# A hybrid decoder layer: ten early weight tiles for the down stage, later token sums, and halves' differences on VectorE

## The chip, the cores and the metric

The kernel runs on one core of one Trainium2 chip, as one launch. The metric is the device time of that launch in microseconds (us); lower is better. A core has five engines that run side by side: TensorE (PE, matmuls into PSUM), VectorE (DVE), ScalarE (ACT), GpSimd (POOL) and SyncE (SP), which here only issues DMAs. DMAs are also issued from GpSimd's queue. All of them share sixteen DMA engines.

## What is computed

One decoder layer on 512 tokens of 1024 channels, in float32. The first sub-layer mixes tokens (RWKV-7 and native sparse attention side by side); the change does not touch it. The second is a gated MLP with a short causal convolution between the up-projection and the gate:

```python
x = x + rms_norm(m @ w_out, norm_mix_post)
h = rms_norm(x, norm_ffn_pre)
u = causal_dwconv(h @ ffn_up, ffn_conv_w, ffn_conv_b)   # width 3, per channel
u_gate, u_val = split(u, 2)                             # 2816 = 22 x 128 each
x = x + rms_norm((silu(u_gate) * u_val) @ ffn_down, norm_ffn_post)
```

## The kernel before

Every matrix is held as a high and a low part (a value rounded to the matmul format, made by a copy on ScalarE, and the rest, made by a subtraction), and each product takes three matmuls: high x high, high x low, low x high. So each weight tile of 128 x 512 costs one DMA of 256 KB into a raw tile, one ScalarE copy (`hi`), one subtraction on VectorE or GpSimd (`lo`), and then its matmuls.

**Up stage** (the loop `for j in range(22)`). Pair j makes 128 gate channels and 128 value channels: two blocks of matmuls, the convolution (one ScalarE and two VectorE instructions for each block, L1619 to L1621), SiLU on ScalarE, the product of both, and its split into `ah[:, j]` (L1638) and `al[:, j]` (L1639). There are two kinds of pairs:

- *Ordinary pairs*, j = 0 to 9: full products with loaded weights (`split_w`, tiles `up..`, line L172 for the rest). The product of gate and value runs on GpSimd (L1630). For j < 11 (`KH`) the right half of the tokens is then replaced by right half less left half (L1637); in ordinary pairs this runs on GpSimd too.
- *Token-half pairs*, j = 10 to 21 (`SEVEN`): a seven-product scheme over halves of the channels and of the tokens (`seven`, L1567 for its matmuls, L1572 for its additions on VectorE, L1578 for its copy). Its weights `sw..` are loaded tiles and sums of tiles that were formed in memory beforehand. Product and difference run on VectorE. For j from 11 on, three more VectorE subtractions make a tile `t24`, which a DMA stores in memory as `t24d[j - 11]` (L1645, the last one from GpSimd's queue, L1652). The pool `t2` that holds `t24` exists from pair 11 to the end of the loop.

**Weight sums** (`ws`): the sums of weight tiles that both seven-product schemes need are formed in memory by DMAs from GpSimd's queue, 48 for the up stage (L251) and then 48 for the down stage (`down_sums`, L272), a plain copy for the first addend and an adding DMA for the second. The generator `ws` is advanced at places written by hand. In the loop above that is once or twice in each ordinary pair and, in token-half pairs, at every even j; in the down stage it is once at every third tile.

**Down stage**: again seven products, `down(m, f, r, n, ..)` for m = 0 to 6, in the order written at the end of the function. Each pass goes over 11 weight tiles (k) and two groups of 128 tokens, three matmuls each (L1730 to L1732). Tiles are numbered n = 0, 1, 2, .. through all passes (`ring`): pass 0 takes 0 to 10, pass 1 takes 11 to 21, and so on; passes 2 to 5 read sums (`ds`). `down_w` allocates and issues a tile: `hi` and `lo` of n = 0 to 2 lie in the ring `whi`/`wlo`, those of later tiles in eight slots of `h2h`/`h2l`, the up stage's input, slot (n - 3) % 8. Raw tiles lie in `wp` (four buffers, shared with the up stage's weights) or in the pool `ep` (four buffers, tag `draw`), which is opened after the pools of the up stage are closed and so lies on their room.

```python
p_, tag, b = (wp, "raw", RAWB) if n < 8 or n % 8 >= 4 else (ep, "draw", 4)
raw = p_.tile([128, 512], F32, tag=tag, name=f"dw{n}r", bufs=b)
load, high = sy.dma_start(raw, src), sc.activation(hi, raw, AF.Copy)
...
low = (po if n % 3 == 1 else ve).tensor_tensor(lo, raw, hi.bitcast(F32), op=OP.subtract)
```

**Token sums** (`turn`): passes 5, 4 and 6 need other token combinations than `ah`/`al` hold. The generator `turn` loads `t24d` back in three chunks of 4, 4 and 3 tiles (L1682; 1024, 1024 and 768 KB), forms for each chunk `ah - t24 + al` in two VectorE instructions (L1690, L1692), and `put` writes the result over `ah` and `al` (L1677 on ScalarE, L1678 on VectorE). It is advanced after the tiles k that `TURN[m]` lists for pass m.

**Order of the work.** The programming layer plans each engine's order with costs of its own; a later instruction can come ahead of an earlier one when its room and inputs are there. `keep` (`tc.keep_in_program_order`) pins an instruction behind everything written before it on its engine. Down tiles from n = 8 on, all chunk loads, sums and `put`s are pinned. Waits for a tile's room are for that tile's former users. Within an engine all runs in order, and a waiting instruction holds up those behind it.

Of the kernel before, what the change touches and what calls it, by code (L numbers as in the profile page):

```python
# [10 lines left out]
F32 = mybir.dt.float32  # L11
F32R = mybir.dt.float32r
AF = mybir.ActivationFunctionType
OP = mybir.AluOpType
# [17 lines left out]
RB = 4  # L32
KH, TL = 11, 4
DCH = tuple(slice(i, min(i + 2, KH)) for i in range(0, KH, 2))
TURN = ((), (0, 4, 6, 7, 8, 10), (1, 3, 4, 6, 8, 9), (3, 6, 9), (2, 5, 8), (), ())
TCH = (slice(0, 4), slice(4, 8), slice(8, 11))
WU = 2
NT = 6
# [14 lines left out]
def hybrid_layer(ctx: ExitStack, tc: tile.TileContext, a, out, dbg=None, stop=None):  # L53
# [1425 lines left out]
    with pool("ff") as ff:  # L1479
# [113 lines left out]
        for j in range(22):  # L1593
            us = []
            sv_ = None
            if j == 2:
                sw = pool("sw", "right", sctx2)
            if j == SEVEN[0]:
                for _ in side:
                    pass  # L1600
            if j in SEVEN:
                sv_ = seven(j)
            for x in range(2):
                blk = 2 * j + x
                if blk < NU:
                    p = pu4[blk]
                    half_up(blk, 1)
                elif sv_ is not None:
                    p = sv_[x]
                else:  # L1610
                    wh, wl = after.get(blk) or split_w(upw(blk), f"up{blk}")
                    p = ((pj, px, py, pz)[blk % 4] if j < SEVEN[0] else pj)(f"pu{blk}")
                    mm3(p, wslice(wh), wslice(wl), lambda k: h2h[:, k, :], lambda k: h2l[:, k, :])
                if blk == 2 * SEVEN[0] - 1:
                    for _ in range(5):
                        next(coming)
                cv = blk * 4
                u = fu.tile([128, S], F32, tag=f"u{x}", name=f"u{blk}", bufs=2)
                sc.activation(u, p, AF.Identity, scale=cvec[:, cv + 2:cv + 3], bias=cvec[:, cv + 3:cv + 4])  # L1619
                ve.scalar_tensor_tensor(u[:, 1:], p[:, :S - 1], cvec[:, cv + 1:cv + 2], u[:, 1:], op0=OP.mult, op1=OP.add)  # L1620
                ve.scalar_tensor_tensor(u[:, 2:], p[:, :S - 2], cvec[:, cv:cv + 1], u[:, 2:], op0=OP.mult, op1=OP.add)  # L1621
                us.append(u)
                if j < SEVEN[0]:
                    for _ in range(1):
                        next(side, None)
                if (j > 2 or x == 0 if j < SEVEN[0] else x + j % 2 == 0):
                    next(ws, None)
            if sv_ is None:
                sc.activation(us[0], us[0], AF.Silu)
                po.tensor_tensor(us[1], us[0], us[1], op=OP.mult)  # L1630
                y = us[1]
            else:
                sc.activation(sv_[0], us[0], AF.Silu)
                y = sv_[1] if j >= KH else us[1]
                ve.tensor_tensor(y, us[1], sv_[0], op=OP.mult)
            if j < KH:
                (po if sv_ is None else ve).tensor_tensor(y[:, rgt], y[:, rgt], y[:, lft], op=OP.subtract)  # L1637
            sc.activation(ah[:, j, :], y, AF.Copy)  # L1638
            ve.tensor_tensor(al[:, j, :], y, ah[:, j, :].bitcast(F32), op=OP.subtract)  # L1639
            if j >= KH:  # L1640
                if j == KH:
                    t2ctx = ExitStack()
                    t2 = pool("t2", "left", t2ctx)
                else:
                    sy.dma_start(t24d[j - 1 - KH], t24)  # L1645
                t24 = t2.tile([128, S], F32, tag="t24", name=f"t24{j}", bufs=2)
                ve.tensor_tensor(t24[:, lft], y[:, rgt], ah[:, j - KH, rgt].bitcast(F32), op=OP.subtract)
                ve.tensor_tensor(t24[:, lft], t24[:, lft], al[:, j - KH, rgt].bitcast(F32), op=OP.subtract)
                ve.tensor_tensor(t24[:, rgt], y[:, lft], t24[:, lft], op=OP.subtract)
            if j == 1:  # L1650
                f4ctx.close()
        po.dma_start(t24d[21 - KH], t24)  # L1652
        t2ctx.close()
        sctx2.close()
        fuctx.close()
        with pool("ep") as ep:
# [23 lines left out]
            def turn():  # L1680
                def load(c):
                    keep(sy.dma_start(t24[:, c], t24d[c].rearrange("k p f -> p k f")))  # L1682

                load(TCH[0])
                yield
                load(TCH[1])
                yield
                for c in TCH:
                    x = ep.tile([128, 4, 256], F32, tag="tt", name=f"tt{c.start}", bufs=1)[:, :c.stop - c.start]
                    keep(ve.tensor_tensor(x, tok(ah, 0, 0, c).bitcast(F32), t24[:, c, lft], op=OP.subtract))  # L1690
                    yield
                    keep(ve.tensor_tensor(x, x, tok(al, 0, 0, c).bitcast(F32), op=OP.add))  # L1692
                    yield
                    put(x, 0, 0, c)
                    yield
                    if c is TCH[0]:
                        load(TCH[2])
                        yield
                for c in TCH:
                    put(t24[:, c, lft], 0, 1, c)  # L1700
                    yield
                for c in TCH:
                    put(t24[:, c, rgt], 1, 0, c)
                    yield

            turned = turn()
            ring = itertools.count()

            def down_w(f, k):
                n = next(ring)  # L1710
                src = a["down4"][f[0], f[1], k] if isinstance(f, tuple) else dsum[k // 2][f][k % 2]
                if n < WB:
                    hi, lo = (wp.tile([128, 512], F32R, tag=t, name=f"dw{t}{n}", bufs=WB) for t in ("whi", "wlo"))
                else:
                    hi, lo = (y[:, (n - WB) % 8, :] for y in (h2h, h2l))
                p_, tag, b = (wp, "raw", RAWB) if n < 8 or n % 8 >= 4 else (ep, "draw", 4)
                raw = p_.tile([128, 512], F32, tag=tag, name=f"dw{n}r", bufs=b)
                load, high = sy.dma_start(raw, src), sc.activation(hi, raw, AF.Copy)  # L1718
                if n >= 8:
                    keep(load)  # L1720
                    keep(high)
                low = (po if n % 3 == 1 else ve).tensor_tensor(lo, raw, hi.bitcast(F32), op=OP.subtract)  # L1722
                if n >= 8:
                    keep(low)
                return hi, lo

            def mms(p, r, n, k, i, w, first, last):
                ks = slice(n * 256 + i * 128, n * 256 + i * 128 + 128)
                xh, xl = (y[:, r * KH + k, ks] for y in (ah, al))
# [4 lines left out]
            def down(m, f, r, n, bank, side=iter(())):  # L1734
                p = [bank(f"dn{m}{i}") for i in range(2)]
                for k in range(KH - TL if m == 6 else KH):
                    w = down_w(f, k)
                    for i in range(2):
                        mms(p[i], r, n, k, i, w, k == 0, k == KH - 1)
                    if k in TURN[m]:  # L1740
# [155 lines left out]
```

## Time and profile before

| | us |
|---|---|
| median of 3 runs | 1151.74 (1150.83 to 1154.2) |
| profiled execution | 1148.3 |
| its span, first to last instruction | 1146.5 |
| TensorE busy | 1116.8 (97%) |
| VectorE busy | 739.3 (64%) |
| ScalarE busy | 639.3 (56%) |
| GpSimd busy | 623.4 (54%) |
| first matmul of the token-half pairs / of the down stage, from the span's start | 900.96 / 1023.25 |

The time is that of a whole launch; the profiled execution is one of its own, and its span leaves out what lies before the first and after the last instruction. In the rows below, "L1722" is line 1722 of the kernel before, `hl<-dw16r,hh` is what an instruction writes and reads, and a bracket at the end of a row says how long its engine stood idle before it and what ended that. In rows by stretch, "PEclk" is the clock that TensorE was granted, as a part of the full one.

### The profile page before, as it was taken

To read this page: it belongs to the slowest core of one execution; us is meant where nothing else is said; L and a number is where in the kernel's file an instruction comes from. 1 tells how busy PE (TensorE), PEld (TensorE's weight loads), DVE (VectorE), ACT (ScalarE), POOL (GpSimd) and SP (SyncE) were. 2 spreads that over 40 slices of the span, in tenths; PEclk is the share of its full clock that TensorE was granted. 3 is DMA by queue.
4 is the path that set the end of the run, shared out by engine and by line. 5 is a ranking of instruction groups with operands and counts; after the bars stand their busy time and mean duration, and the time that the engine had idled before them with its cause. 6 is when DMAs were issued, how large, how long until landed. Compare 5 with 4: busy or idle time off the path is not lost.

```text
span 1146.5 us, 21236 instructions
## 1 busy us (share of the span) xinstructions
PE 1116.8 (97%) x7704; PEld 910.9 (79%) x7704; DVE 739.3 (64%) x1420; ACT 639.3 (56%) x1258; POOL 623.4 (54%) x627
## 2 busy tenths in 40 slices
PE   9999999999999999999999999999999999998997
PEld 7888888777888787666676778889778899996685
DVE  4236655735665653687787745754873699986886
ACT  6447764554666334576775554444454567654644
POOL 4346765545765554566555535531678877743331
PEclk9999999999999999999999999999999999999999
DMA  7524568543665897336575466685558677879583
GB/s 265 138 72 122 154 169 226 149 121 96 183 145 172 236 255 194 95 105 185 182 196 174 111 165 194 200 300 132 161 166 200 214 227 226 241 192 312 191 288 116
DMA packets 117002, 208.33 MB, mean 182 GB/s; under 512 B 37025, under 2 KB 39905, under 8 KB 110754
## 3 DMA queue, kind: packets, MB, share of 16 engines
q1 hardware_dynamic: 93538, 144.05, 39.9%
q0 software_dynamic: 7504, 48.50, 18.5%
q10 hardware_dynamic: 15856, 14.42, 4.0%
q8 instruction: 61, 1.00, 0.3%
q14 instruction: 43, 0.35, 0.1%
HBM read 179.60 MB, written 72.35 MB: 220 GB/s over the span
## 4 chain that ended last, share of the span: by engine, by line
PE 81%; DVE 7%; DMA 4%; POOL 4%; ACT 3%; issue 2%; SPq 0%; ACTq 0%; DVEq 0%; POOLq 0%
PE sg L1567 4%; PE st L1567 4%; PE gt L348 3%; PE o L1218 3%; PE gt L349 3%; PE gt L350 3%; PE pt L150 3%; PE ub L1276 3%; PE ub L1278 2%; PE ub L1277 2%; PE pu L234 2%; PE pu L232 2%; PE pu L233 2%; PE v L348 2%; PE v L349 2%; PE dn L1731 2%
## 5 line engine op out<-in xcount | busy, mean ns | idle before, releaser
L1166 ACT ACTIVATE p<-p,stt 128x384 f32<-128x384 f32 (+3 forms) x128 | 70.6, 554 | 33.6 <-DVE stt L1164 33.0
L1164 DVE CUSTOM_DVE_ANT_0 p<-s,rh 128x384 f32<-128x384 f32 (+3 forms) x128 | 59.2, 484 | 22.0 <-PE s L1150 18.4
L1731 PE MATMUL dn<-hl,ah 128*128 128x512 f32 x148 | 59.3, 401 | 2.9 <-POOL hl L1722 1.5
L1138 POOL TENSOR_SCALAR p<-p,stt 128x512 f32<-128x512 f32 (+1 forms) x64 | 39.5, 626 | 38.8 <-DVE stt L1131 24.0
L1730 PE MATMUL dn<-hh,ah 128*128 128x512 f32 x148 | 57.5, 395 | 2.8 <-ACT hh L1718 2.7
L1732 PE MATMUL dn<-hh,al 128*128 128x512 f32 x148 | 58.3, 394 | 0.0
L150 PE MATMUL pt<-ident,p 128*128 128x128 f32 x320 | 44.3, 273 | 1.3 <-DVE p L1140 1.2
L1157 PE MATMUL s<-kst,qs 128*128 128x512 f32 (+1 forms) x128 | 38.8, 394 | 6.0 <-DVE stt L1164 5.8
L150 PEld LDWEIGHTS pt<-ident,p 128*128 128x128 f32 x320 | 37.8, 141 | 6.9 <-DVE p L1140 1.6
L1218 PE MATMUL o<-PT,vt 128*64 128x384 f32 (+3 forms) x256 | 41.0, 443 | 0.0
L1731 PEld LDWEIGHTS dn<-hl,ah 128*128 128x128 f32 x148 | 28.2, 190 | 12.1 <-DVE hl L1722 3.9
L1730 PEld LDWEIGHTS dn<-hh,ah 128*128 128x128 f32 x148 | 27.8, 189 | 10.3 <-ACT hh L1718 4.7
L1209 ACT ACTIVATE PT<-pt 128x512 f32<-128x512 f32 x48 | 27.5, 587 | 10.4 <-PE pt L150 10.3
L1157 PEld LDWEIGHTS s<-kst,qs 128*128 128x128 f32 x128 | 21.2, 189 | 15.2 <-DVE stt L1164 11.9
L1732 PEld LDWEIGHTS dn<-hh,al 128*128 128x128 f32 x148 | 28.2, 191 | 5.6
L1140 DVE TENSOR_SCALAR p<-p,stt 128x512 f32<-128x512 f32 (+1 forms) x64 | 31.9, 526 | 0.7
L1218 PEld LDWEIGHTS o<-PT,vt 128*64 128x64 f32 x256 | 16.4, 136 | 18.3 <-issue 16.0
L1638 ACT ACTIVATE ah<-u 128x512 fp32r<-128x512 f32 x11 | 7.0, 632 | 40.9 <-POOL u L1637 40.6
L272 POOL DMA_DIRECT2D ds<-in_down_dram x36 | 25.6, 711 | 6.9 <-DMA ds<-ds 6.0
L1211 DVE COPY PT<-pt 128x512 f32<-128x512 f32 x32 | 21.7, 680 | 8.6 <-PE pt L150 8.5
L1639 DVE TENSOR_TENSOR al<-u,ah 128x512 fp32r<-128x512 f32 x11 | 9.2, 837 | 26.5 <-ACT ah L1638 26.5
L251 POOL DMA_DIRECT2D fs<-in_up_dram x36 | 26.1, 731 | 0.5 <-issue 0.4
(2203 smaller groups left out, 4247.0 us busy)
## 6 DMA issues: line engine op xcount, KB each, us to landing
fs<-in_up_dram POOLq DMA_DIRECT2D x36, 512.0 KB, 6.2
ds<-in_down_dram POOLq DMA_DIRECT2D x30, 512.0 KB, 6.0
fs<-fs POOLq DMA_DIRECT2D x12, 512.0 KB, 4.5
ds<-ds POOLq DMA_DIRECT2D x10, 512.0 KB, 5.1
gtd<-gt ACTq DMA_DIRECT2D x16, 256.0 KB, 3.5
qs<-qd SPq DMA_DIRECT2D x32, 128.0 KB, 3.8
g<-gtd SPq DMA_DIRECT2D x16, 256.0 KB, 3.4
t24d<-t SPq DMA_DIRECT2D x10, 256.0 KB, 4.9
```

What stands on the lines that cost most here:

```text
L150: return te.transpose(o, i, ident)
L348: te.matmul(p, wh(k), hh[:, k, :], start=k == 0, stop=False)
L349: te.matmul(p, wh(k), hl[:, k, :], start=False, stop=False)
L1138: po.tensor_scalar(o.pe[e, b, k], o.pe[e, b, k], w, 1.0, op0=OP.mult, op1=OP.mult)
L1157: m = te.matmul(s_[:, :n], qt, kt[:, x, b, :n], start=x == 0, stop=x == 1)
L1164: ve.tensor_tensor_reduce(sb, parts[b], rh[e][:, (3 - qb) * 128:], -1.0, BIG, OP.add, OP.min, st[e][:, 0, i:i + 1])
L1166: sc.activation(sb, sb, AF.Exp, scale=-1.0, bias=st[e][:, 0, i:i + 1], accum_out=st[e][:, 1, i:i + 1])
L1218: te.matmul(acc[e * 64:e * 64 + 64, j * 128:], vt[:, j, b * 256 + g * 64:b * 256 + g * 64 + 64], m[e][:, c:c + n], start=False, stop=k == ...
L1567: te.matmul(p, w[y][:, ks], x[z][:, k, :], start=first and k + n == 0, stop=last and k == hf - 1 and n == 2, skip_group_check=True)
L1730: te.matmul(p, xh, w[0], start=first, stop=False)
L1731: te.matmul(p, xh, w[1], start=False, stop=False)
L1732: te.matmul(p, xl, w[0], start=False, stop=last)
```

## The change

Four things:

1. `down_w` moves to the end of the up stage, ahead of the closing of its pools, and the first ten tiles are issued there (`begun`). Tiles 8 and 9 get raw room in `t2` (two buffers) instead of `ep`; from n = 10 on, tiles with n % 8 of 2 to 5 use `ep`'s four buffers, the others `wp`. Pinning begins at n = 10 instead of 8.
2. `TURN`: the chunk loads, sums and `put`s come later, and the two instructions of a sum are one step. Chunk loads go out after tiles 14, 19 and 23 (before: 11, 15 and 21), the sums after 20, 25 and 29 (before: their first instructions after 17, 23 and 28), the first `put`s after 22, 27 and 31 (before 19, 26 and 31).
3. In token-half pairs `ws` is advanced at every j from 10 to 18 instead of at even j from 10 to 20. Nine down sums are left at that point.
4. In ordinary pairs the difference of the token halves runs on VectorE; in pairs 8 and 9 the product does so too.

```diff
-TURN = ((), (0, 4, 6, 7, 8, 10), (1, 3, 4, 6, 8, 9), (3, 6, 9), (2, 5, 8), (), ())
+TURN = ((), (3, 8, 9), (0, 1, 3, 5, 7, 9), (2, 5, 8), (2, 5, 8), (), ())
...
-                if (j > 2 or x == 0 if j < SEVEN[0] else x + j % 2 == 0):
+                if (j > 2 or x == 0 if j < SEVEN[0] else x == 0 and j < 19):
                     next(ws, None)
             if sv_ is None:
                 sc.activation(us[0], us[0], AF.Silu)
-                po.tensor_tensor(us[1], us[0], us[1], op=OP.mult)
+                (ve if j > SEVEN[0] - 3 else po).tensor_tensor(us[1], us[0], us[1], op=OP.mult)
...
             if j < KH:
-                (po if sv_ is None else ve).tensor_tensor(y[:, rgt], y[:, rgt], y[:, lft], op=OP.subtract)
+                ve.tensor_tensor(y[:, rgt], y[:, rgt], y[:, lft], op=OP.subtract)
...
         po.dma_start(t24d[21 - KH], t24)
+        ring = itertools.count()
+
+        def down_w(f, k):
...
+            if n < 8 or n > 9 and n % 8 < 2 or n % 8 >= 6:
+                raw = wp.tile([128, 512], F32, tag="raw", name=f"dw{n}r", bufs=RAWB)
+            elif n < 10:
+                raw = t2.tile([128, 512], F32, tag="draw", name=f"dw{n}r", bufs=2)
+            else:
+                raw = ep.tile([128, 512], F32, tag="draw", name=f"dw{n}r", bufs=4)
+            load, high = sy.dma_start(raw, src), sc.activation(hi, raw, AF.Copy)
+            low = (po if n % 3 == 1 else ve).tensor_tensor(lo, raw, hi.bitcast(F32), op=OP.subtract)
+            if n >= 10:
+                keep(load)
+                keep(high)
+                keep(low)
+            return hi, lo
+
+        begun = [down_w((0, 0), k) for k in range(10)]
         t2ctx.close()
...
                     keep(ve.tensor_tensor(x, tok(ah, 0, 0, c).bitcast(F32), t24[:, c, lft], op=OP.subtract))
-                    yield
                     keep(ve.tensor_tensor(x, x, tok(al, 0, 0, c).bitcast(F32), op=OP.add))
...
             def down(m, f, r, n, bank, side=iter(())):
                 p = [bank(f"dn{m}{i}") for i in range(2)]
                 for k in range(KH - TL if m == 6 else KH):
-                    w = down_w(f, k)
+                    w = begun.pop(0) if begun else down_w(f, k)
```

More of the change, by code (lines that the diff above doesn't have):

```diff
@@ L1652, in hybrid_layer @@
         po.dma_start(t24d[21 - KH], t24)
+        ring = itertools.count()
+        def down_w(f, k):
+            n = next(ring)
+            src = a["down4"][f[0], f[1], k] if isinstance(f, tuple) else dsum[k // 2][f][k % 2]
+            if n < WB:
+                hi, lo = (wp.tile([128, 512], F32R, tag=t, name=f"dw{t}{n}", bufs=WB) for t in ("whi", "wlo"))
+            else:
+                hi, lo = (y[:, (n - WB) % 8, :] for y in (h2h, h2l))
+            if n < 8 or n > 9 and n % 8 < 2 or n % 8 >= 6:
+                raw = wp.tile([128, 512], F32, tag="raw", name=f"dw{n}r", bufs=RAWB)
+            elif n < 10:
+                raw = t2.tile([128, 512], F32, tag="draw", name=f"dw{n}r", bufs=2)
+            else:
+                raw = ep.tile([128, 512], F32, tag="draw", name=f"dw{n}r", bufs=4)
[7 more added lines that the diff above has]
+        begun = [down_w((0, 0), k) for k in range(10)]
         t2ctx.close()
@@ L1706, in hybrid_layer @@
             turned = turn()
[L1707 to L1725, printed above, removed]
             def mms(p, r, n, k, i, w, first, last):
```

## The prediction

> **What bounds the kernel now.** I read the span and shares first, then what the TensorE waited for, then stretches of 5 us, then single rows where a stretch was not full.
>
> ```profile
> span 1146.5 us, 21236 instructions
> PE st L1567 <- DVE sv L1572: 2.2, 1, 2.2
> PE pu L234 <- POOL up5l L172: 1.7, 1, 1.7
> PE pu L234 <- POOL up10l L172: 0.4, 1, 0.4
> PE dn L1730 <- ACT hh L1718: 2.7, 2, 2.2
> ```
>
> These are the span and, for two windows (760 to 960 us and 960 us to the end), the waits of the TensorE: total, times, longest. TensorE is the bound almost everywhere; what the change can win is the little time in which it stands still, and the clock it then loses.
>
> ```profile
> core 0: us, PE busy (x) PEld busy (x) DVE busy (x) ACT busy (x) POOL busy (x), PEclk, DMA share, GB/s
> 905.00:910.00 5.00, 4.48 (x39) 4.28 (x38) 3.78 (x1) 0.59 (x2) 4.30 (x4) 1.00 0.93 272
> 910.00:915.00 5.00, 3.31 (x20) 3.31 (x21) 4.63 (x8) 3.68 (x8) 4.35 (x5) 0.80 0.54 160
> 915.00:920.00 5.00, 5.00 (x39) 5.00 (x38) 3.67 (x8) 3.22 (x6) 2.68 (x3) 0.85 0.81 301
> 918.00:1023.00 105.00, 104.63 (x896) 104.05 (x895) 100.01 (x167) 72.47 (x125) 73.35 (x58) 1.00 0.75 220
> 975.00:980.00 5.00, 4.79 (x41) 4.59 (x41) 4.76 (x10) 3.92 (x8) 3.04 (x3) 1.00 0.94 270
> 1045.00:1050.00 5.00, 2.17 (x7) 1.16 (x7) 0.68 (x1) 1.93 (x4) 1.28 (x1) 0.96 1.05 396
> 1050.00:1055.00 5.00, 4.97 (x16) 4.03 (x17) 4.48 (x4) 1.46 (x3) 1.74 (x1) 0.70 1.04 376
> 1070.00:1075.00 5.00, 4.16 (x18) 3.05 (x17) 2.99 (x4) 2.46 (x5) 1.27 (x1) 1.00 0.47 150
> 1075.00:1080.00 5.00, 4.16 (x17) 2.47 (x16) 3.32 (x6) 2.80 (x7) 1.00 (x1) 1.00 0.40 107
> ```
>
> In the rows by stretch the columns are busy time (and instructions) of TensorE, its weight loads, VectorE, ScalarE and GpSimd, then the granted clock and the DMA share. Three places stand out: the change from ordinary to token-half pairs (905 to 920), where TensorE stops and then runs at a clock of 0.80 and 0.85; the down stage at 1045 to 1055, where it stops with the DMA engines full (1.05) and then gets 0.96 and 0.70; and 1070 to 1080, where DMA is not full. In the token-half pairs (918 to 1023) TensorE is full, but VectorE is busy 100.0 of 105 us: nothing may be added to it there.
>
> ```profile
> 1023.25 0.40 PE L1730 MATMUL dn<-dwwhi,ah 128*128 128x512 f32 x1
> 1033.92 0.39 PE L1732 MATMUL dn<-hh,al 128*128 128x512 f32 x1
> 1138.51 0.39 PE L1732 MATMUL dn<-hh,al 128*128 128x512 f32 x1
> ```
>
> These are the first, the 48th and the last matmul of the down stage. The first 48 are 10.67/47 = 0.227 us apart. The stage has 7 passes x 11 tiles x 2 x 3 = 462 of them, which at that pace take 104.9 us; from the first start to the last end at that pace it took 115.5. So 10.6 us are lost there, and no gain in the stage can exceed that. By the distances from start to start over those 462 rows, about 5.8 of it lies between 1043 and 1053 (1.7 of this is clock: 5 x 0.04 + 5 x 0.30), 3.9 between 1066 and 1080, 0.9 elsewhere.
>
> **The change, part by part.**
>
> *Token sums later, ten early tiles.* A down tile is loaded, rounded on ScalarE, its rest subtracted on VectorE or GpSimd (tile n with n%3 = 1), then used six times by TensorE, 1.36 us per tile.
>
> ```profile
> 1028.78 0.33 SPq L1718 DMA_DIRECT2D dw8r<-in_down_dram  x1
> 1030.64 0.38 SPq L1682 DMA_DIRECT2D t<-t24d  x1
> 1033.60 0.44 SPq L1682 DMA_DIRECT2D t<-t24d  x1
> 1034.78 0.33 SPq L1718 DMA_DIRECT2D dw16r<-in_down_dram  x1
> 1035.14 0.83 POOL L272 DMA_DIRECT2D ds<-in_down_dram  x1
> 1047.98 0.63 ACT L1718 ACTIVATE hh<-dw16r 128x512 fp32r<-128x512 f32 x1 [3.73 <-DMA dw16r<-in_down_dram]
> 1048.69 1.28 POOL L1722 TENSOR_TENSOR hl<-dw16r,hh 128x512 fp32r<-128x512 f32 x1 [7.64 <-ACT hh L1718]
> ```
>
> From the issue of tile 8 to the arrival of tile 16 are 19.2 us; on SP's queue this carried tiles 8 to 16 (9 x 256 KB) and two token chunks of 1024 KB (8 tiles' worth), beside the store of the last token rows and one weight sum on GpSimd's queue. That is 19.2/17 = 1.13 us per tile's worth. TensorE at its pace wants tile 16 at 1023.25 + 16 x 1.363 = 1045.1, so it should have landed 1.9 us earlier (0.63 + 1.28), at 1043.2. It landed 4.8 us late, which is the stall with its clock loss. After the change tiles 8 and 9 sit in a pool that exists since pair 11, so they are loaded before 1028.78; the first chunk is queued behind tile 14 instead of 11, the second behind 19 instead of 15, and the sum at 1035.14 is gone. Ahead of tile 16's arrival then stand tiles 10 to 16 and one chunk, 11 tiles' worth: 11 x 1.13 = 12.4, so 1041.2, 2.0 us early. Tile 20 is next in danger, behind 11 tiles and both chunks: 19 x 1.13 = 21.5, so 1050.3, where 1050.5 less 1.3 (20 goes over VectorE) = 1049.2 is wanted: 1.1 late at that crowded rate. At 396 GB/s (row 1045) 19 tiles take 12.6 us and it is 8 early. I take no stall at 16 and 0.5 at 20.
>
> The DMAs moved: two loads come earlier on SP's queue (into 918 to 1023, share 0.75), three chunk loads stand in SP's queue 3, 4 and 2 tiles later (the third moves from behind tile 21 to behind 23). Nothing needs the chunks soon: their sums feed pass 5. SP's wait for tile 10's room (formerly tile 8's) holds up only the tiles behind it; tile 10 is wanted at 1036.9.
>
> The sums themselves: putting a chunk back overwrites what pass 1 reads. Before, the first was queued behind tile 19, now behind tile 22; rounding tile 22 waits for room that tile 14 leaves, which is the same moment at which the chunk's old rows are free, so the extra wait is gone. VectorE has the same work, 2.4 us for a sum of two, 1.2 for a rest.
>
> ```profile
> 1071.93 0.60 ACT L1388 ACTIVATE p2jk<-dn 128x512 f32<-128x512 f32 x1 [5.05 <-DVE res L1386]
> ```
>
> That ScalarE wait of 5.05 us, with the rounding of tiles 31 and on queued behind it, is the loss at 1066 to 1080: VectorE arrived there late because it had sat idle at 1045 (0.68 of 5 us). Freed of that it comes about 5 us earlier; I take 1.0 of the 3.9 as left, because a whole put-back (1.2) moves from pass 1 into pass 2. The stage in sum: of 10.6, left are 0.5 at tile 20, 1.0 late, 0.9 small ones: gain 8.2. Ends: 4.0 (only half of the first loss, a little of the second) and 10.6; a loss is excluded only by the same work on the same queues, so I keep zero as a far end for the rival below.
>
> *Weight sums of the down stage earlier.* Before, they go out at pairs 10, 12, .. 20 and three more in pass 0; now at pairs 10 to 18, nine in a row. The last six add into memory.
>
> ```profile
> 971.69 0.81 POOL L272 DMA_DIRECT2D ds<-in_down_dram  x1
> 973.05 1.33 DVE L172 TENSOR_TENSOR sw178l<-sw178r,sw178h 128x512 fp32r<-128x512 f32 x1 [0.16 <-ACT sw178h L134]
> 977.66 0.28 PE L1567 MATMUL sv<-tf0h,sw171l 128*128 128x256 f32 x1
> 978.15 0.39 PE L1567 MATMUL st<-tf2h,sw173h 128*128 128x256 f32 x1 [0.21 <-DVE su L1572]
> ```
>
> An adding sum holds GpSimd for 0.81 us, its next subtraction then runs beside VectorE's, which takes 1.33, and TensorE starts 0.49 after its predecessor where 0.12 is usual: 0.37 lost. The one at 991.67 does the same. Four more of them fall into these pairs (13, 14, 15, 17): 4 x 0.37 = 1.5 lost. Ends: 0, since the sum at pair 20 cost TensorE nothing, and 3.0 (each doubled, because six at 10 us each keep the DMA share near the 0.94 of row 975).
>
> *Differences and products to VectorE, ordinary pairs.*
>
> ```profile
> L1637 POOL TENSOR_TENSOR u<-u x10: 728/740/1189, 808.5 to 908.3; 128x256 f32<-128x256 f32 x10
> L1637 DVE TENSOR_TENSOR u<-u x1: 416/416/416, 919.6 to 919.6; 128x256 f32<-128x256 f32 x1
> 903.28 0.75 DVE L1621 SCALAR_TENSOR_TENSOR u<-pu,cvec,u 128x510 f32<-128x510 f32 x1
> 904.42 1.31 POOL L172 TENSOR_TENSOR sw115l<-sw115r,sw115h 128x512 fp32r<-128x512 f32 x1
> 904.59 4.19 DVE L172 TENSOR_TENSOR sw111l<-sw111r,sw111h 128x512 fp32r<-128x512 f32 x1
> 906.93 1.29 POOL L1630 TENSOR_TENSOR u<-u,u 128x512 f32<-128x512 f32 x1
> 908.30 1.08 POOL L1637 TENSOR_TENSOR u<-u 128x256 f32<-128x256 f32 x1
> 909.41 0.63 ACT L1638 ACTIVATE ah<-u 128x512 fp32r<-128x512 f32 x1 [4.85 <-POOL u L1637]
> 911.21 0.43 DVE L1572 TENSOR_TENSOR sv<-st,su 128x256 f32<-128x256 f32 x1
> 911.69 0.39 PE L1567 MATMUL st<-tf3h,sw108h 128*128 128x256 f32 x1 [2.21 <-DVE sv L1572]
> ```
>
> Ten differences leave GpSimd (740 ns) for VectorE (416 ns), and the products of pairs 8 and 9 too (GpSimd 1.29; on VectorE twice the 256-wide 0.42 less its start, some 0.7). In pairs 2 to 8 TensorE never waits, so this is worth nothing; the cover is two blocks of matmuls ahead, and VectorE's own wait for the rounding shortens as it takes on 0.42. At pair 9 it is on the path: both GpSimd steps are queued behind other subtractions, rounding and rest follow, then the addition at 911.21 that TensorE waits for. Its last start before was at 909.21, so 2.4 us are lost, and the clock of 0.80 and 0.85 afterwards costs 5 x 0.20 + 5 x 0.15 = 1.75 more. Now the product can start at 904.1, when both its inputs are there. If VectorE is held by GpSimd's two subtractions in a row until 907.0, product and difference end at 908.1, rounding at 908.7, rest 909.4, the two additions 910.3, and 1.0 of 2.4 stays, without the clock loss: gain 3.1. If it isn't held, all 4.1. If the planner leaves VectorE's 4.19 us subtraction ahead, it ends near 907.7, the additions near 911, and 0.5 is left. I take 3.1; ends 0.5 and 4.1.
>
> [...]
>
> The wait of 1.7 at pair 2's weights (TensorE behind GpSimd's up5l) hangs on GpSimd's product, which waits for VectorE; the difference before it shortens the chain by 0.74 - 0.42 = 0.3, and GpSimd has 0.7 less to do: gain 0.5, ends -0.5 (VectorE's added 0.42 in front) and 1.7. The 0.4 at up10l comes straight behind a difference of 1.19 on GpSimd: gain 0.4, ends 0 and 0.7.
>
> **Sum.** 8.2 - 1.5 + 3.1 + 0.5 + 0.4 = 10.7 us. The profiled execution took 1148.3 (span 1146.5), so 1137.6 by its own time. It stands 3.4 below the median of the three runs, 1151.74; against those 1141.0.
>
> **The rivals.**
> *The jam only moves* (DMA). For it: shares of 1.04 to 1.05, and tile 20's margin is negative at the crowded rate. Against: a sum and two tiles leave the crowd. Then the first loss of 5.8 stays, and 4.9 is left: 1146.8.
> *VectorE is held at pair 9* as the 4.19 us row shows, and the other two waits stay: 3.5 less, gain 7.2, 1144.5.
> *The clock dips come anyway.* In rows: the dips at 913 and 1050 follow stops of 2.4 and 2.6 us, and after the stop at 817 none came; had they another cause, 1.75 + 1.7 would stay: gain 7.3, 1144.4. [...]
> *The change doesn't do what it says*: tiles 8 and 9 are queued no earlier and the new VectorE steps just change places with others. Gain 0 to 2, say 1150.7.
> *Slower: six adding sums in a row* in the token-half pairs, where VectorE has 5 us to spare in 105 and DMA is at 0.94 after each. If weights came late by more than their buffers cover, each sum would stop TensorE. To be slower than before by 3.5 it must cost (10.7 + 1.5 + 3.5)/6 = 2.6 us per sum, seven times what it costs now; at 3 us each the time is 1151.7 + 18 - 12.2 = 1157.5.
>
> **How the numbers follow.** A difference of 0.3%, 3.5 us, is about what a measurement of this kernel can tell from none. Chances: forecast 0.52; held at pair 9 0.13; clock 0.04; jam moves 0.11 (half of it within 0.3%, as 1146.8 is close to the border of 1148.3); no effect 0.11; sums 0.09, the rest of small mishaps counted in. Faster 0.52 + 0.13 + 0.04 + 0.06 = 0.75, same 0.05 + 0.11 = 0.16, slower 0.09. The range goes from 1136.0 (stage 10.6, sums 0, pair 9 4.1, the rest 1.0) to 1149.5, so that the slower cases and part of "no effect" lie outside.
>
> **What would show it.** Right: no wait of `dn` on tile 16, granted clock 1.00 from 905 to 1080; last `dn` start some 110 us or less behind the first; no TensorE wait for `sv` at the tenth pair; no sum (L272) after the token-half pairs. Wrong: DMA share still over 1 where tiles 16 to 20 land, a wait of TensorE of 0.5 us and more in each of pairs 13 to 18, or VectorE's subtraction still at 4 us beside GpSimd at pair 9.

## The result, and the profile after

| kernel | median, us | ratio to the kernel before, 95% interval |
|---|---|---|
| before, beside the first set | 1151.47 (6 runs) | 1 |
| changed, first set | 1144.26 (6 runs) | 0.9936 [0.9911, 0.9960] |
| changed, second set (before: 1151.6) | 1146.06 (7 runs) | 0.9943 [0.9920, 0.9966] |

The change gains 7.2 and 5.5 us, some 6.4 where 10.7 were forecast; 1141.0 was too low, the range holds both sets. The profiled execution of the changed kernel took 1146.95 us, the slowest of its six, that of before 1148.3, faster than its median. They differ by 1.4 us only, because the changed kernel's run reached its first up-projection matmul 3.57 us later (790.17 against 786.60), 2.3 us of it within the first 12 us. TensorE's order of work is the same up to there, so that is a difference between runs. From that matmul to the last one of the down stage it is 346.8 us after and 351.9 before: 5.1 us less.

The page's span and TensorE's waits in the same two windows, after:

```profile
span 1144.9 us, 21224 instructions
PE st L1567 <- DVE su L1572: 4.2, 4, 2.4
PE pu L234 <- POOL up5l L172: 0.7, 1, 0.7
PE dn L1734 <- DVE hl L1669: 1.3, 3, 0.6
PE dn L1733 <- ACT hh L1668: 1.1, 2, 0.7
PE dn L1734 <- POOL hl L1669: 0.6, 1, 0.6
```

and before, beside the rows that the prediction shows, in the second window:

```profile
PE dn L1731 <- POOL hl L1722: 1.5, 2, 0.8
PE dn L1731 <- DVE hl L1722: 1.3, 3, 0.7
```

The waits for `sv` and `up10l` are gone, that for `up5l` fell from 1.7 to 0.7. The waits of the down stage (`dn`) fell from 5.5 us in all to 3.0, the longest of them from 2.2 to 0.7. New are 4.2 us for `su` in the first window, 2.4 of them in one wait. By stretches, columns as before:

```profile
core 0: us, PE busy (x) PEld busy (x) DVE busy (x) ACT busy (x) POOL busy (x), PEclk, DMA share, GB/s
905.00:910.00 5.00, 3.62 (x31) 3.43 (x31) 4.96 (x7) 1.84 (x5) 2.51 (x3) 1.00 0.79 277
910.00:915.00 5.00, 5.00 (x46) 5.00 (x45) 2.47 (x5) 3.23 (x5) 4.48 (x5) 1.00 0.76 206
918.00:1023.00 105.00, 101.36 (x860) 99.97 (x859) 98.16 (x165) 70.68 (x124) 70.49 (x58) 1.00 0.78 228
925.00:930.00 5.00, 3.61 (x32) 3.41 (x30) 4.77 (x6) 1.77 (x5) 1.64 (x2) 1.00 0.70 245
1045.00:1050.00 5.00, 5.00 (x24) 4.14 (x23) 1.38 (x2) 3.02 (x6) 2.08 (x2) 1.00 1.05 395
1050.00:1055.00 5.00, 5.00 (x24) 4.14 (x23) 4.63 (x4) 2.14 (x4) 1.56 (x1) 1.00 0.95 351
1070.00:1075.00 5.00, 3.62 (x13) 2.02 (x12) 3.21 (x4) 2.18 (x5) 1.29 (x1) 1.00 0.34 103
1075.00:1080.00 5.00, 4.30 (x18) 3.15 (x18) 3.95 (x4) 5.00 (x10) 2.51 (x2) 1.00 0.59 163
```

At 1045 to 1055 TensorE is full at a clock of 1.00, although the DMA engines are nearly as full as before (1.05 and 0.95). That share over 1 was one of the prediction's signs of being wrong; it came, and cost TensorE nothing. Three places are left: 905 to 910, a new stop at 925 to 930, and 1070 to 1080, in its first half worse than before (3.62 against 4.16). In the last, GpSimd is busy 1.29 and 2.51 of 5 us and the DMA engines have a share of 0.34 and 0.59, so neither is full there.

Tile 16's rounding, the first and the last matmul of the down stage:

```profile
1026.73 0.40 PE L1733 MATMUL dn<-dwwhi,ah 128*128 128x512 f32 x1
1043.80 0.63 ACT L1668 ACTIVATE hh<-dw16r 128x512 fp32r<-128x512 f32 x1 [1.28 <-DMA dw16r<-in_down_dram]
1136.94 0.39 PE L1735 MATMUL dn<-hh,al 128*128 128x512 f32 x1
```

Tile 16 comes 17.1 us after the first matmul (24.7 before), and the last start lies 110.2 us behind the first (115.3 before).

To compare kernels whose spans are shifted, the span is cut at four first matmul starts: of `up5h` (pair 2), `sw125` (pair 12), `sw205` (pair 20), `dn`; the last column goes to the last start of `dn`. Without any loss that column is 461 distances of 0.227 = 104.7 us. All times are in us; a ratio is against the kernel before, run beside that kernel:

| kernel | parts of the change | median | ratio [interval] | up5h to sw125 | sw125 to sw205 | sw205 to dn | down stage |
|---|---|---|---|---|---|---|---|
| before | none | | 1 | 108.18 | 79.18 | 19.45 | 115.26 |
| changed | room, sums, VectorE | 1144.26 | 0.9936 | 104.29 | 83.00 | 19.44 | 110.21 |
| e9 | the same again | 1146.06 | 0.9943 | 104.42 | 83.87 | 19.44 | 110.16 |
| e1 | room, VectorE | 1147.74 | 0.9973 [0.9956, 0.9990] | 104.50 | 79.79 | 25.70 | 113.76 |
| e2 | room | 1151.38 | 1.0001 [0.9980, 1.0022] | 106.86 | 79.93 | 21.62 | 113.27 |
| e3 | VectorE | 1148.69 | 0.9981 [0.9964, 0.9999] | 104.42 | 80.42 | 19.44 | 114.49 |
| e5 | sums | 1148.10 | 0.9952 [0.9934, 0.9970] | 106.84 | 84.16 | 19.44 | 109.08 |
| e11 | sums, VectorE | 1145.98 | 0.9953 [0.9936, 0.9970] | 104.41 | 85.47 | 19.44 | 108.87 |
| e4 | all, sums placed otherwise | 1141.45 | 0.9914 [0.9891, 0.9937] | 103.78 | 79.98 | 19.44 | 109.41 |
| e6 | all, first token sum earlier | 1146.28 | 0.9947 [0.9930, 0.9964] | 104.41 | 86.55 | 19.48 | 106.67 |
| e10 | the same again | 1144.52 | 0.9938 [0.9918, 0.9959] | 104.42 | 87.91 | 19.48 | 108.25 |
| e7 | all, norm later | 1144.57 | 0.9924 [0.9906, 0.9942] | 104.44 | 84.79 | 19.44 | 105.98 |
| e8 | e4, e6 and e7 together | 1137.87 | 0.9865 [0.9848, 0.9881] | 103.78 | 80.72 | 19.44 | 104.52 |
| e12 | e4 and e7, without room | 1143.52 | 0.9926 [0.9903, 0.9949] | 103.80 | 79.52 | 20.55 | 107.69 |

"Room" is the ten early tiles with the later token sums (parts 1 and 2 of the change), "sums" part 3, "VectorE" part 4. The stretches are of one profiled run each, the medians of 4 to 12. The changed kernel has -3.9 us in the first column, +3.8 in the second, -5.05 in the fourth: -5.1 in all.

### The profile page after: what moved, and what is told of

It is laid out like the page before. It is cut to its first block, busy times and chain, and to the rows that moved or that the text cites. A ratio compares the mean times of both kernels' runs of the same rounds, so it can differ in the third digit from the quotient of the medians.

```text
span 1144.9 us, 21224 instructions
## 1 busy us (share of the span) xinstructions
PE 1116.2 (97%) x7704; PEld 910.2 (79%) x7704; DVE 747.6 (65%) x1432; ACT 640.1 (56%) x1258; POOL 608.5 (53%) x615
## 4 chain that ended last, share of the span: by engine, by line
PE 80%; DVE 7%; DMA 4%; POOL 3%; issue 3%; ACT 2%; DVEq 0%; POOLq 0%; ACTq 0%; SPq 0%
PE sg L1567 4%; PE st L1567 4%; PE o L1218 3%; PE gt L348 3%; PE pt L150 3%; PE ub L1276 3%; PE pu L234 2%; PE gt L349 2%; PE ub L1278 2%; PE gt L350 2%; PE pu L233 2%; PE pu L232 2%; PE ub L1277 2%; PE v L348 2%; PE v L349 2%
## 5 line engine op out<-in xcount | busy, mean ns | idle before, releaser
L1157 PEld LDWEIGHTS s<-kst,qs 128*128 128x128 f32 x128 | 21.2, 189 | 15.5 <-DVE stt L1164 12.3
L1620 DVE SCALAR_TENSOR_TENSOR u<-pu,cvec,u 128x511 f32<-128x511 f32 x20 | 15.0, 748 | 20.4 <-ACT u L1619 20.4
L868 ACT ACTIVATE UV<-xs 64x256 f32<-64x256 f32 x16 | 6.1, 378 | 35.6 <-PE xs L861 35.2
```

The lines of the kernel that those rows point to most:

```text
L1157: m = te.matmul(s_[:, :n], qt, kt[:, x, b, :n], start=x == 0, stop=x == 1)
```

## The experiments

### Which part brings what

*e1: the changed kernel with the weight sums where they were.*

```diff
-                if (j > 2 or x == 0 if j < SEVEN[0] else x == 0 and j < 19):
+                if (j > 2 or x == 0 if j < SEVEN[0] else x + j % 2 == 0):
```

> The changed kernel with the weight sums where they were before: after every second pair of the token halves as well, three of them left for the down stage. Theory A (a sum's issue on GpSimd pushes its rounding subtraction sw?4l onto VectorE's sw?8l, the two exclude each other, and VectorE is late for the pair): the 2.51 us stop of TensorE at 928 us goes, the intervals from sw125 to sw205 become 3.8 us shorter; the three sums that return to the first pass of the down stage cost at most 1.5 us there, since its tiles now have their buffers early. Time 2 to 4 us under the changed kernel, 1140.5 to 1142. Rival B (the sums' placement costs nothing, the 2.51 us are of the run): the intervals stay within 1 us of the changed kernel's, time 1143 to 1146. Rival C (the sums in the first pass are what lost time before): 3 to 6 us are lost between the first down matmul and 1055 us, time 1146 or more.

Theory A's stretch came out (79.79, 3.2 less than 83.00), its time did not. 1147.74 is in C's range, but not by C's place: only 1.3 us are lost between the first down matmul and 1055. The sums that return cost 6.3 us at the end of the pairs (25.70 against 19.44) and 3.5 in the whole down stage, more than their absence in the pairs saves. This profile's run (1153.79) is the slowest of twelve and shows the bad case. Rows of GpSimd, SP's queue, ScalarE and TensorE of e1:

```profile
1012.59 0.77 POOL L272 DMA_DIRECT2D ds<-in_down_dram  x1
1012.68 0.33 SPq L1668 DMA_DIRECT2D dw3r<-in_down_dram  x1
1019.30 0.63 ACT L1668 ACTIVATE hh<-dw3r 128x512 fp32r<-128x512 f32 x1 [3.92 <-DMA dw3r<-in_down_dram]
1019.84 0.76 ACT L1619 ACTIVATE u<-sv,cvec 128x512 f32<-128x512 f32 x1
1021.76 0.58 PE L1567 MATMUL st<-tf2h,sw213h 128*128 128x256 f32 x1 [2.78 <-DVE su L1572]
```

and the stretch behind it:

```profile
1020.00:1025.00 5.00, 3.23 (x15) 3.24 (x16) 3.53 (x7) 3.02 (x6) 3.02 (x2) 0.60 0.13 31
```

The sum of pair 20 (512 KB) and down tile 3 are issued in the same 0.1 us; the tile takes 6.6 us to be rounded (2.7 without the sum, in the changed kernel: issue 1015.19, rounding 1017.91). Its rounding stands on ScalarE ahead of the last pair's convolution, so TensorE, in the up stage still, is held by a weight tile of the down stage: 2.78 us and a clock of 0.60. By this the early room needs the sum out of pair 20; that edit alone was not run.

*e2: the kernel before with the room alone* (`TURN`, `down_w` and `begun` of the change, nothing else).

> The kernel before with the down stage's part alone: ten weight tiles begun early, token sums later; weight sums, product and differences as before. If the parts add up as the two traces have it (down stage -5.1, pairs before the down stage -3.9, sums +3.8), the pairs cost what they did before and the down stage is 3 to 5 us shorter than before: 1146 to 1148.5. Rival (the jam is the returning sums', not the tiles' room): down stage as before within 1 us, 1150.5 to 1152.

No gain at all: 1.0001. The jam is gone here too (0.7 us lost at 20 to 30 us into the stage, where before loses 5.65), so the rival is wrong on that, though the time is in its range. But 2.2 us go at the last pairs, where a sum and down tile 3 are again issued together (1016.20 and 1016.29), and behind the jam's place it loses 7.9 us where before loses 4.6.

*e3: the kernel before with the work on VectorE alone* (the two lines of part 4).

> The kernel before with the change of engine alone: differences of ordinary pairs on VectorE, products of the last two ordinary pairs too. As the intervals of the two traces have it: up5h to sw125 3.9 us shorter, of it 1.9 at the tenth pair and the clock dip after it and 2.0 at the up weights of the pairs before; down stage unchanged: 1147 to 1148.5. Rival (the clock dip at the tenth pair comes anyway, and a shorter stage only meets a fuller down stage): 1150 to 1152.

2.5 us, just over the expected 1148.5. The profile's 3.8 in the first column holds a dip of the granted clock that only some runs have: e2 and e5 stop at the same place without VectorE's part and take 106.85, so the part itself is worth 2.4, and the measured time agrees.

*e5: the kernel before with the sums moved, alone.*

> The kernel before with the weight sums' part alone (a sum after each of the pairs 11 to 18, none after the last three pairs, none left for the down stage). Theory A (cost in the pairs, gain only together with the early room, which needs the transfers of the last pairs free): the stretch from sw125 to sw205 becomes 2.5 to 3.8 us longer, the down stage 0 to 2 us shorter, since its tiles 14 to 17 still wait for buffers: 1151 to 1154. Rival C (the three sums in the first pass were the jam at 1043 to 1053 us): the down stage 4 to 6 us shorter, 1147 to 1149.

Rival C, with theory A's price in the pairs (+5.0) beside it: the down stage is 6.2 us shorter with no early room. The ten-microsecond stretches from ten before the first down matmul on, before:

```profile
1013.25:1023.25 10.00, 10.00 (x89) 10.00 (x88) 9.17 (x16) 6.08 (x11) 4.50 (x5) 1.00 0.81 175
1023.25:1033.25 10.00, 10.00 (x47) 8.26 (x46) 6.97 (x13) 4.84 (x8) 1.30 (x1) 1.00 0.77 230
1043.25:1053.25 10.00, 6.85 (x21) 4.40 (x20) 4.62 (x4) 3.53 (x6) 3.03 (x2) 0.83 1.05 393
```

and of e5, the same distances from its first down matmul (1032.04):

```profile
1022.04:1032.04 10.00, 10.00 (x89) 10.00 (x88) 9.85 (x20) 6.58 (x12) 2.56 (x2) 1.00 0.46 140
1032.04:1042.04 10.00, 10.00 (x47) 8.26 (x45) 7.96 (x14) 5.25 (x9) 2.42 (x3) 1.00 0.77 249
1052.04:1062.04 10.00, 9.88 (x43) 7.70 (x42) 8.74 (x8) 6.44 (x12) 3.96 (x4) 1.00 0.71 258
```

Tile 16's issue and its rounding in e5:

```profile
1041.16 0.33 SPq L1718 DMA_DIRECT2D dw16r<-in_down_dram  x1
1050.57 0.63 ACT L1718 ACTIVATE hh<-dw16r 128x512 fp32r<-128x512 f32 x1 [2.81 <-DMA dw16r<-in_down_dram]
```

Tile 16 is rounded 18.5 us after the first down matmul (1050.57 - 1032.04), with the same pools and the same chunk loads ahead of it; before it was 24.7, in time is 19.9. DMA was at 0.81 ahead of the stage for the sums, now at 0.46. Rows of SP's queue show how that reaches tile 16: the last store of token rows from that queue before, then the same store and tile 8 in e5:

```profile
1024.18 0.33 SPq L1645 DMA_DIRECT2D t24d<-t  x1
```

```profile
1031.17 0.33 SPq L1645 DMA_DIRECT2D t24d<-t  x1
1033.62 0.33 SPq L1718 DMA_DIRECT2D dw8r<-in_down_dram  x1
```

Tile 8's raw room (`ep`) is that of the closed pools of the up stage, and in both runs its issue comes 0.02 us after this store has landed. Before, the store was issued 0.9 us after the first down matmul and took 4.6 us, so tile 8 went out at 5.5 us (1028.78); in e5 it was issued 0.9 us ahead of that matmul and took 2.4, so tile 8 went out at 1.6. Tile 16's own load then took 13.1 us from issue to landing before and 9.3 in e5. Three of the four sums that e5 moves had been issued 11.6, 3.5 and 0.9 us ahead of the first down matmul, the last two of them though the program has them in the first pass; the fourth came 0.4 us behind the issue of tile 16. By these rows the three made the store late and the fourth lengthened the load, but no run moves them one by one. In e2 (room alone) tile 16 is rounded 20.6 us after the first down matmul, in the changed kernel 17.1. Each part alone brings tile 16 in time or nearly so; the two together bring it 2.8 us early, which is worth nothing.

*e11: sums and VectorE, no room*, and beside it *e9, the changed kernel again*.

> The kernel before with the weight sums moved and the work on VectorE, but without the down stage's early room and with the token sums in their old places. Theory E (moving the sums out of the first pass already ends the jam, the early room gives nothing more and makes the late passes 1.8 us worse): its down stage is 108.5 to 109.5 us, as in the run with the sums alone, and the time 1 us under the changed kernel to equal, 1143 to 1145. Theory of the prediction (room for tiles 14 to 17 is what pays): the down stage 112 or more, time 1147 to 1149.

> The changed kernel once more, unedited, beside the other three of this call: it says how far the median of one and the same kernel moves between sets of runs, and whether its stop at the thirteenth pair (2.5 us at 928 us) brings a lower granted clock, as it did in the profiles of the sums alone (sw125 to sw135 13.98 us), of the early first sum (13.87) and of the later norm (13.83), but not in the changed kernel's own profile (12.36). If the clock dip belongs to the stop: 13.8 to 14.0 here. If the two are unrelated: 12.4. Time 1143 to 1146.

1145.98 against 1146.06: within the intervals of some 2 us the time is the same without the two parts of the change that the forecast's 8.2 us stood on. Its down stage is 1.3 us shorter than e9's. Theory E holds, though both times lie 1 us above its figures. In e9 the stop at the thirteenth pair came again, the dip (13.8 to 14.0) did not: 12.26.

### The new stop at the thirteenth pair (j = 12)

GpSimd, VectorE, ScalarE and TensorE of the changed kernel:

```profile
923.55 0.52 POOL L272 DMA_DIRECT2D ds<-in_down_dram  x1
924.09 1.31 POOL L172 TENSOR_TENSOR sw124l<-sw124r,sw124h 128x512 fp32r<-128x512 f32 x1
925.35 1.29 POOL L172 TENSOR_TENSOR sw135l<-sw135r,sw135h 128x512 fp32r<-128x512 f32 x1
923.72 3.48 DVE L172 TENSOR_TENSOR sw128l<-sw128r,sw128h 128x512 fp32r<-128x512 f32 x1 [0.16 <-ACT sw128h L134]
928.23 0.78 ACT L1619 ACTIVATE u<-sv,cvec 128x512 f32<-128x512 f32 x1 [3.23 <-DVE sv L1572]
930.39 1.29 POOL L172 TENSOR_TENSOR sw132l<-sw132r,sw132h 128x512 fp32r<-128x512 f32 x1 [3.76 <-ACT sw132h L134]
930.96 0.39 PE L1567 MATMUL st<-tf2h,sw123h 128*128 128x256 f32 x1 [2.35 <-DVE su L1572]
```

The sum's issue holds GpSimd for 0.52 us; its subtraction `sw124l` then starts 0.37 us after VectorE's `sw128l` and `sw135l` follows without a gap. VectorE's subtraction lasts through both and ends at 927.20, 0.6 us after the second; then its chain reaches TensorE 2.4 us late. GpSimd idles for 3.76 us right behind. The profiles split cleanly on this: in the seven with the stop `sw128l` starts 0.26 to 0.37 us ahead of `sw124l` and takes 3.4 to 3.5 us; in the other seven, that of before among them, `sw124l` starts first, by 0.23 to 1.27 us, and `sw128l` takes 1.0 to 1.6.

*e4: the sum's issue into that idle time, behind the fifth subtraction instead of ahead of the fourth.*

```diff
             prod(v[:, rgt], forms[0])
+            if SEVEN[0] < j < 20:
+                next(ws, None)
             add(u4, v[:, rgt], u2)
...
-                if (j > 2 or x == 0 if j < SEVEN[0] else x == 0 and j < 19):
+                if j < SEVEN[0] and (j > 2 or x == 0):
```

> The changed kernel with as many weight sums in the token halves' pairs, each issued behind its pair's fifth weight subtraction (in GpSimd's idle time) instead of ahead of the fourth. Theory A (the sum's issue delays sw?4l onto VectorE's sw?8l): the stop of 2.51 us at 928 goes, the intervals from sw125 to sw205 become 2.5 to 3.8 us shorter, 1140.5 to 1142. Rival D (the sums' transfers crowd the weights of the pair): as many bytes in the same stretch, so the loss stays within 1 us: 1143.5 to 1145.

Theory A: 1141.45, 3.0 us less between sw125 and sw205. GpSimd and VectorE of e4:

```profile
920.29 1.75 POOL L172 TENSOR_TENSOR sw124l<-sw124r,sw124h 128x512 fp32r<-128x512 f32 x1
921.41 1.18 DVE L172 TENSOR_TENSOR sw128l<-sw128r,sw128h 128x512 fp32r<-128x512 f32 x1 [0.16 <-ACT sw128h L134]
922.77 1.30 POOL L172 TENSOR_TENSOR sw135l<-sw135r,sw135h 128x512 fp32r<-128x512 f32 x1 [0.73 <-ACT sw135h L134]
924.01 0.52 POOL L272 DMA_DIRECT2D ds<-in_down_dram  x1
```

`sw128l` takes 1.18 instead of 3.48, beginning under the first GpSimd subtraction and over before the second, with as many sums in the same pairs. D may have a small share: a stop of 1.40 us at 967 came behind a weight tile (`sw168r`) that ScalarE awaited for 2.56 us. In e12, with its sums in the same places, that stop is 0.27, so the size is open.

### The loss that stayed in the second and third pass

ScalarE's rounding of tile 20, VectorE and ScalarE of the changed kernel:

```profile
1049.66 0.63 ACT L1668 ACTIVATE hh<-dw20r 128x512 fp32r<-128x512 f32 x1 [1.93 <-DMA dw20r<-in_down_dram]
1050.32 0.69 DVE L1669 TENSOR_TENSOR hl<-dw20r,hh 128x512 fp32r<-128x512 f32 x1 [3.36 <-ACT hh L1668]
1050.93 1.22 DVE L1714 TENSOR_TENSOR tt<-ah,t 128x1024 f32<-128x1024 f32 x1
1069.19 0.60 ACT L1388 ACTIVATE p2jk<-dn 128x512 f32<-128x512 f32 x1 [5.09 <-DVE res L1386]
1069.78 0.62 ACT L1668 ACTIVATE hh<-dw31r 128x512 fp32r<-128x512 f32 x1
```

VectorE stands idle 3.36 us for tile 20, because its first token sum is pinned behind that tile; the sum's chunk was issued at 1033.72. It is then late for `res`, ScalarE's square waits 5.09 us for that, and the rounding of tile 31 is pinned behind the square. Two edits, each on the changed kernel:

```diff
 # e6: first sum behind tile 18, ahead of the second chunk's load
-TURN = ((), (3, 8, 9), ...
+TURN = ((), (3, 7, 8), ...
...
                 load(TCH[0])
                 yield
-                load(TCH[1])
-                yield
                 for c in TCH:
...
                     yield
+                    if c is TCH[0]:
+                        load(TCH[1])
+                        yield
                     put(x, 0, 0, c)
...
 # e7: residual add and squares a pass later
-            p5 = down(2, 0, 0, 1, pz, first_half(p2))
-            p4 = down(3, 3, 1, 1, pj)
+            p5 = down(2, 0, 0, 1, pz)
+            p4 = down(3, 3, 1, 1, pj, first_half(p2))
```

> The changed kernel with the first token sum behind tile 18 and ahead of the second chunk's load, instead of behind tile 20. T1 (VectorE is late in the passes after because it stands idle 3.4 us for tile 20, behind which its first sum is pinned): the idle time is filled, VectorE is some 3 us earlier at res, the 5.2 us that TensorE loses at 1067 to 1086 us fall to 2 to 3: 1141.5 to 1142.5. T2 (ScalarE's square p2jk stands ahead of the rounding of tile 31, and the square waits for the whole chain of sums and norm): the same chain ends some 3 us earlier, so 1 to 2 us are left at that place. T3 (too much VectorE work in these two passes, whatever the order): under 1 us gained, 1143.5 to 1144.5.

> The changed kernel with the first token sum ahead of tile 20, once more. Its profile showed the down stage 3.5 us shorter than the changed kernel's (106.67 against 110.21), its median of 1146.28 was 2 us above that of another set. If the 3.5 us are real and the rest was a difference of the pairs between runs, it is 2 to 4 us under the changed kernel of this call; if something that the profile does not show takes them back, within 1 us of it or above.

> The changed kernel with the norm's first half (residual add and squares) beside the fourth pass instead of the third; VectorE's idle time at tile 20 stays. T2 and T3 (the square pinned ahead of tile 31's rounding, or the work piled up in the second and third pass): the loss of 5.2 us at 1067 to 1086 us falls below 2, 1140.5 to 1141.5, if the end does not become later by the norm itself. T1 alone (VectorE late by its idle time, whatever comes behind): 3 us or more are left there, 1142.5 to 1144. A rival that ends higher: the norm's later result is needed ahead of the last pass, and the end moves by up to 5 us.

By the distances from start to start, 40 to 60 us into the stage, the changed kernel loses 5.6 us (the expectations have 5.2); e6 keeps 2.1 of it, e10 3.7, e7 1.4. The earlier first sum alone wins 2 to 3.5, so T3, too much work in any order, falls; T1's idle time and T2's square pinned ahead of tile 31 both have a part. In time neither moved beyond the intervals: e6 (1146.28) and e7 (1144.57) lie above all the times expected of them from the stage, e10 is 1.5 us under e9 where 2 to 4 or at most 1 were expected. For e6 and e10 the stretch sw125 to sw205 was 3.6 and 4.9 us longer than in the changed kernel's first profile, a part of it in the waits for `su` at pairs 16 and 19 (1.16 and 1.52 us in e6, 1.46 and 2.50 in e10, 0.43 and 0.35 in the changed kernel). The instructions stand in the same order there as in the changed kernel, and e9, e7 and e11, where they do too, took 0.9, 1.8 and 2.5 us longer. So some of it is a difference between runs; whether all is, stays open. In e7 the profile's last matmul starts 8.6 us ahead of the span's end, 0.6 more than in the changed kernel.

*e8: e4, e6 and e7 together.*

> The changed kernel with three edits together: weight sums behind the fifth weight subtraction (1141.45 by itself), first token sum behind tile 18, norm's first half a pass later. If the parts add up: 1141.45 less the 4 to 5 us of the late passes, 1136.5 to 1138. If the sum ahead of the norm's move leaves nothing for the other (both treat the same 5.2 us), still 1137 to 1138.5; if the late passes' loss only moves to the fourth pass, 1140 to 1142.

1137.87, 0.9865: this is the fastest version, 1.35% under the kernel before, and in the range of parts that add up. By the medians, though, e6 and e7 alone gave next to nothing, and with e4 they give 3.6 us more than e4. Its down stage has no loss (104.52). By stretches:

```profile
1045.00:1050.00 5.00, 5.00 (x24) 4.14 (x23) 4.27 (x5) 3.31 (x5) 2.93 (x2) 1.00 1.05 385
1070.00:1075.00 5.00, 5.00 (x23) 4.13 (x23) 5.00 (x6) 1.91 (x4) 2.02 (x2) 1.00 0.97 316
1075.00:1080.00 5.00, 5.00 (x23) 4.13 (x22) 3.69 (x6) 1.73 (x4) 1.30 (x1) 1.00 0.42 121
```

*e12: the same without the early room* (and with the token sums in their old places).

> The kernel before with the work on VectorE, the weight sums behind the fifth weight subtraction and the norm's first half a pass later, without the early room and with the token sums in their old places. If the early room is worth nothing even there: 1136.5 to 1138.5, as the best version with it (1137.87). If it pays once the late passes are cleared: 1139 to 1142.

1143.52, 5.6 above e8 and above both figures expected. TensorE loses 3.0 us in the stage, and the end comes 12.6 us behind the start of the last matmul instead of 8.1. The addition of the last chain's beginning on VectorE, in e12:

```profile
1123.23 0.68 DVE L1753 TENSOR_TENSOR pa<-dn,pa 128x512 f32<-128x512 f32 x1
```

and in e8:

```profile
1118.10 0.68 DVE L1757 TENSOR_TENSOR pa<-dn,pa 128x512 f32<-128x512 f32 x1
```

It starts 5.1 us later where the last matmul is 1.7 later (1129.97 against 1128.29): VectorE sets the end. The chain of work that ended last names `dw63r` (7.43 us of DMA) before it; that wasn't tried. e12 lacks the early first sum of e8 too, so the difference isn't shown to be the room's alone. It leaves open that the room pays once the other losses are gone.

## Why the prediction was partly right

The direction and the range held; the reason given for most of the gain was wrong.

- **The step that failed: the jam was put down to the tiles' room and the chunks' place, and the weight sums were priced only for what they cost in the pairs.** The text counted 17 tiles' worth from the issue of tile 8 on and mentioned "one weight sum" beside them. It took that issue, 5.5 us into the stage, as given; the sums issued just before the stage, which held the store that tile 8 waited for, were left out. e5 shows the jam gone without room (down stage -6.2), e11 that room adds nothing to sums and VectorE, e2 that room alone gains nothing. The forecast's +8.2 for parts 1 and 2 is about 0 in this kernel, its -1.5 for part 3 is a gain of 5.5 (e5's ratio; 3.5 to 7.6 by its interval).
- Tile 16: landed 17.1 us behind the first matmul, forecast 18.0 (1041.2 - 1023.25). Tile 20: 22.9, between the two estimates (27.1 and 18 by rate); TensorE lost nothing there, as against 0.5.
- The late loss: 1.0 taken as left, 5.6 measured, more than the 4.0 before (3.9 in the forecast's own count). The step "freed of that it comes about 5 us earlier" overlooked that the sums now stand behind tile 20, for which VectorE waits 3.36 us.
- Weight sums in the pairs: 1.5 taken, 3.0 as the end; 3.8 and 4.7 in the changed kernel's two profiles, 5.0 in e5, and 5.6 to 8.7 in e7, e11, e6 and e10, where the order of work is the same. The size was wrong because the row chosen (0.37 a sum) had no GpSimd subtraction following without a gap. Stops of half a microsecond in each pair, named as the sign of this rival, didn't come; one of 2.4 did. Spread over the six adding sums of that rival, even 8.7 us is under 1.5 each; its 2.6 was not reached.
- Pair 9: 3.1 taken. sw105 to sw125 is 23.66 before and 21.71 after, 1.95; without the clock dip, which e2 (22.25) and e5 (22.26) don't have, 0.5. VectorE was held: its product took 2.43 us under two GpSimd subtractions, and TensorE waits 1.38 us for `su` now. That was the rival with 0.13; that its time, 1144.5, is nearly the measured one is luck, as it kept the 8.2 of the down stage.
- `up5l` and `up10l`: 0.5 and 0.4 taken; up5h to up10h 1.05 shorter, up10h to sw105 0.89. (The wait at `up10l` is in pair 5, so TensorE did wait in pairs 2 to 8.) With pair 9 that makes 3.9 where 4.0 were taken in all, which is luck too: the sizes were wrong in both directions, and 1.4 of the 3.9 is a dip that only some runs have.
- The clock: 1.00 from 905 to 1080 in the changed kernel's profile. That rival fell, but the 1.75 us that the forecast counted for the dip at pair 9 were no steady gain: e2 and e5 have the stop there without the dip.

The order on GpSimd mattered: with the same instructions and another place of one DMA issue, `sw128l` takes VectorE 1.18 us in e4 and 3.48 in the changed kernel. There such a subtraction takes 0.68 us where none of GpSimd's runs beside it (`sw111l`, `sw121l`). The row of 3.48 us starts 0.37 us ahead of GpSimd's `sw124l` and lasts through that and the next (1.31 and 1.29), so both of GpSimd's were over before a VectorE instruction that had begun ahead of either. In the same way the row of 4.19 us of before lay under four of GpSimd's (1.31, 1.29, 1.29 and the first 0.48 of 1.08). Once VectorE was ahead and GpSimd took longer: in the changed kernel `sw108l` starts 0.03 us before GpSimd's `sw104l`; they take 0.69 and 1.82.

## What to carry to other kernels

When a tile comes late, ask what its queue was waiting for before the first of the late loads went out, and count every transfer on the shared engines back to there, those of other queues and other stages too: what freed the down stage (-6.2 us in e5) was another queue's work, taken out of its first pass and the last pairs ahead of it. Two remedies for one jam need not add up, so measure each alone before the sum is believed. A sum's issue held GpSimd for 0.52 to 0.81 us in the changed kernel's token-half pairs; what it cost the kernel was decided by the instruction behind it (`sw128l` took 3.48 us there and 1.18 in e4), so put it in front of a gap and not in front of the instruction that another engine must not meet.

## What was not expected of the hardware

The same stop brings a lower granted clock in some runs and not in others. The stretch behind the stop at the thirteenth pair (a wait of 2.25 us in both), in e11:

```profile
930.00:935.00 5.00, 4.78 (x27) 4.79 (x28) 4.97 (x9) 2.03 (x5) 3.78 (x4) 0.66 0.54 159
```

and in e9:

```profile
930.00:935.00 5.00, 5.00 (x46) 5.00 (x45) 4.83 (x9) 3.06 (x5) 4.33 (x4) 1.00 0.68 185
```

Of the seven profiles that have this stop, those of e5, e6, e7 and e11 show the dip (sw125 to sw135 13.8 to 14.0 us), those of the changed kernel, e9 and e10 don't (12.3 to 12.4); it costs 1.6 us. e6 and e10 are one and the same kernel. The dip of before at pair 9 was of the same kind, and one profile can't price it. What decides whether such a stop brings the dip, no run shows; the length of the wait doesn't, being the same in e11 and e9.
